# Token sums of the output projection: eight router products and four sums of squares per group of four blocks instead of three products per block

## The chip, the cores and the metric

The kernel runs on one NeuronCore of one Trainium2 chip. The metric is the device time of one execution in microseconds; the median of three runs of the kernel before is 2050.81 us (2050.77, 2050.81 and 2059.14).

## The reference, cut to what matters

Two layers (`DEPTH = 2`) work on 256 context tokens and 256 latent tokens of width 1024. Each layer has a token mixer, which ends in an output projection, and an expert-choice mixture of 16 experts. What the experts need of a token is its root mean square and its router affinity, both sums over all 1024 channels of the stream that leaves the mixer:

```python
def rms_norm(x, g):
    xf = x.astype(jnp.float32)
    y = xf * lax.rsqrt(jnp.mean(xf * xf, axis=-1, keepdims=True) + EPS)
    return (y * g.astype(jnp.float32)).astype(x.dtype)

def modulate(x, g, shift, scale):
    return rms_norm(x, g) * (1 + scale) + shift

def expert_choice_moe(h, router, w1, w3, w2):
    cap = CAPACITY_FACTOR * L // N_EXPERTS
    aff = jax.nn.softmax((h @ router).astype(jnp.float32), axis=-1)
    g, idx = lax.top_k(aff.transpose(0, 2, 1), cap)
    ...
```

The second layer drops the context, so its mixer and its experts end in 256 tokens where the first has 512.

## The kernel before, in words

The stream x is held transposed: a block is 128 channels on the partitions, with 512 tokens (context and latents) in the free dimension, or 256 in the second layer. There are KB = 8 such blocks.

**Output projection** (lines 1356 to 1376). For each block d, `load` (line 791) brings the 128 columns `wo{d}` of the output matrix, 512 KB, into one of three raw buffers, ScalarE copies its high part (L798) and VectorE subtracts to get the low part (L799), into one of two pairs of buffers. TensorE then runs 24 products, three for each of eight k, into a PSUM tile of tag "d" (`pd` in the rows): 128x512 in the first layer, 128x256 in the second. VectorE adds the result, times the modulation, to x (L1372), once for each stream. Then `pre.step(d)` takes what the experts need of this block.

**Token sums** (`TokenSums`, line 534, used by `MoePre`, line 587). For block k, `step` issues one router product for each stream, [128 channels, 32] against x, 256 tokens, into 32 partitions of PSUM tile `pr` (`pm` in the rows); a square of x on ScalarE (L550); and one product of a matrix of ones with the square, 512 or 256 tokens, into 32 partitions of PSUM tile `p2` (`pa` in the rows). Which 32 partitions, and with it which column group of the array, depends on the block:

```python
q, r = (k % 4, 4) if ns == 1 else (2 * s + k % 2, 2)
j = 32 * (k % 4)
```

These products are plain float32, which the trace shows as two rows each. `tokens` (line 553) copies both tiles out (L558, L560) and adds the four groups up in small products. From there VectorE makes 1/rms, softmax and top-k (L576, L500 to L504, L1399 to L1424), and the gather of the experts' tokens starts. The same class runs once more, without a router, at the end of the first layer's experts (L1657 and L1659), for the norm of the second mixer; its `p2` has tag "s" there (`ps` in the rows).

**Experts** (`moe`, line 1386). Their weights come as 384 tiles of 1 MB (two of the last matrix by columns), issued by SyncE in one queue (L1565), first come first served, into whatever buffers are free; a tile is issued when the products that read the buffer before are done. Some buffers are free during the output projection, six in a region that was just given back, others when the projection's own operands and x's helpers are released. The DMAs of `wo{d}` (L797) are in the same queue.

Matmuls of all helpers are recorded at L428, transposes at L425. The order of each engine's instructions is set by a scheduler from the program and its own estimate of times, not by hand.

Of the kernel before, what the change touches and what calls it, by code (L numbers as in the profile page):

```python
# [19 lines left out]
KB = 8  # L20
NE = 16
CAP = 32
EPS = 1e-6
RA, RB = 12288, 12288                            # columns of the two regions that change type with the phase
BASE = 52736 - RA - RB
ENGS = ('AV', 'AVG')                             # engines of the copies of q and k, by layer
# steps of the modulation (by layer, of which parts may be left over) among the other work
TR = (0, 2, 0.5)                                 # at the end of the experts, before and among the second mixer's h
SCN = (0.5, 0.5)                                 # per level of a scan
FL = (1, 1)                                      # the rest before the merge  # L30
DAS = (0.5, 1)                                   # per head and query block
ADA = (2, 2)                                     # per block of w_in
FIRST = ("gk", "gq")                             # blocks of the second mixer loaded during the experts
AHEAD = ((0, 0), (0, 5))                         # tiles of experts loaded during the mixers


# ---------------------------------------------------------------- layouts
# [21 lines left out]
LATE = CN.at["adab"][0]                          # those from here on give way to weights of the experts  # L59
C0 = Pack()                                      # needed at the start only  # L60
# [104 lines left out]
def dft():  # L165
    """Transforms at the odd frequencies 2 pi (k + 1/2) / 512, k < 256, where no wrapped term meets the 511 of the
    convolution. Phases are counted from the middles of the signal, 127.5, of the filter's tap 128, and of the
    outputs 128..383; cosines are then even and sines odd in t <-> 255 - t, and half of the t will do."""
    th = 2 * np.pi * (np.arange(256) + 0.5) / 512
    a = np.outer(np.arange(256) - 128, th)  # L170
    filt = np.concatenate([np.cos(a), -np.sin(a)], 1)
    a = np.outer(np.arange(128) - 127.5, th)
    fwd = np.concatenate([np.cos(a), -np.sin(a)], 1)
    inv = np.concatenate([np.cos(a.T), np.sin(a.T)], 1) / 256
    two = lambda m: m.reshape(2, 128, -1).transpose(1, 0, 2).reshape(128, -1)
    return np.concatenate([two(filt), fwd, two(inv)], 1).astype(np.float32)


def pack_inputs(a):
    """Layout of the inputs; every element is a copy of an input's element or a constant of the shapes."""  # L180
# [50 lines left out]
    for l in range(2):  # L231
# [5 lines left out]
        wb = a["w_branch"][l].reshape(4, 2, 128, 2, 4, 128)          # i, k, p, half, d, n  # L237
        for i in range(4):
            for h in range(2):
                wg[l, BIDX[f"wb{i}{h}"]] = wb[i, :, :, h].transpose(1, 2, 0, 3).reshape(128, 8, 128)   # p, (d, k), n  # L240
# [10 lines left out]
# ---------------------------------------------------------------- device  # L251
class Mem:
    """Columns of one SBUF tile, those longest free first; Tile sees which bytes each instruction touches."""
# [7 lines left out]
    def take(self, n, avoid=None):  # L261
        """avoid: first and last + 1 of columns not to be touched."""
# [39 lines left out]
    def merge(self):  # L302
        """Joins neighbouring free runs (their stamps become the latest)."""
# [8 lines left out]
    def cut(self, b, n):  # L312
        """Gives the first n columns of b back; the rest stays."""
# [12 lines left out]
class Buf:  # L326
# [3 lines left out]
    def __call__(self, off=0, dims=None, p0=0, np_=128, n=None):  # L330
        """AP of rows p0..p0+np_, from column off, free dims [[stride, count], ...]."""
# [19 lines left out]
def build(tc, ins, outT, dbg=None, stop=None):  # L351
# [30 lines left out]
    # ---------------- persistent  # L382
    cn = mem.take(CN.n)
    sm = mem.take(SM.n)                              # of the layer
    cs_b = mem.take(256)
    mod = [mem.take(96) for _ in range(2)]          # [6 chunk, 8 k, 2 stream]
    xb = [mem.take(4096), 0]                         # [stream, k, 256]; columns cut off in front
    x_at = xb[0].at
    NR = 3
    raws = [mem.take(1024) for _ in range(NR)]       # blocks of the mixers' weights as they come  # L390
# [45 lines left out]
    # ---------------- adaLN  # L436
    def load_c(c):
        """silu(c) of both streams, 32 columns for each block of 128."""
# [17 lines left out]
    class Ada:  # L456
        """Streams ada_w[l] in tiles of one k-block of a 1024-column chunk."""
# [17 lines left out]
    class AdaBack:  # L475
        """The same in the background, in two buffers of its own."""
# [6 lines left out]
        def run(self, n=None):  # L483
            """n: steps, or parts of one."""
# [12 lines left out]
    # ---------------- little helpers  # L497
    def rsqrt_small(x, n, y, t):
        """y = x ** -0.5 on n columns (x, y, t: functions of nothing giving APs)."""
# [6 lines left out]
    def rms_rows(l, t0, mem=mem, nsq=3):  # L506
        """1/rms over d of x, on every partition: PSUM [128, 512 - t0]."""
# [26 lines left out]
    class TokenSums:  # L534
        """Sums over d while x comes block by block: x^2, and x against a [d, 16] matrix per stream."""
# [6 lines left out]
        def step(self, k):  # L542
            W, b, ns = 512 - self.t0, self.sq[k % len(self.sq)], self.ns
            j = 32 * (k % 4)
            if self.AR:
                for s in range(ns):
                    ss = s + 2 - ns
                    q, r = (k % 4, 4) if ns == 1 else (2 * s + k % 2, 2)
# [1217 lines left out]
```

## Time and profile before

| | |
|---|---|
| median of three runs | 2050.81 us |
| span of the profiled execution, first to last instruction | 2046.6 us |
| the median less that span | 4.2 us |
| TensorE matmul busy | 1883.5 us (92%) |
| VectorE busy | 801.6 us (39%) |
| ScalarE busy | 525.8 us (26%) |
| bytes moved by DMA | 549.03 MB, mean 268 GB/s |

The profile comes from one execution; beside its span no further time of that execution is recorded, so the 4.2 us around it are the difference to the median run. A busy TensorE means that a matmul is in the pipeline, not that it is used to the full. Rows of the trace give the start in microseconds from the first instruction, the length, engine, source line, operation, out<-in by the program's names, the shape (rows*columns of the array, then the operand that streams through), and how many instructions the row merges. A float32 product is two such instructions, a product of the projection's split parts one.

### The profile page before, as it was taken

To read this page: it belongs to the slowest core of one execution; us is meant where nothing else is said; L and a number is where in the kernel's file an instruction comes from. 1 tells how busy PE (TensorE), PEld (TensorE's weight loads), DVE (VectorE), ACT (ScalarE), POOL (GpSimd) and SP (SyncE) were. 2 spreads that over 40 slices of the span, in tenths; PEclk is the share of its full clock that TensorE was granted. 3 is DMA by queue.
4 is the path that set the end of the run, shared out by engine and by line. 5 is a ranking of instruction groups with operands and counts; after the bars stand their busy time and mean duration, and the time that the engine had idled before them with its cause. 6 is when DMAs were issued, how large, how long until landed. Compare 5 with 4: busy or idle time off the path is not lost.

```text
span 2046.6 us, 28476 instructions
## 1 busy us (share of the span) xinstructions
PE 1883.5 (92%) x11722; PEld 1091.5 (53%) x11722; DVE 801.6 (39%) x1768; ACT 525.8 (26%) x929; POOL 27.4 (1%) x52
## 2 busy tenths in 40 slices
PE   7999999999999799999887899999998999997877
PEld 3666677887886434434232356888996433231213
DVE  5455648747442323212120245769864111010101
ACT  4433336622231211101000243447442100000000
POOL 0000000000000000000000010001000000000000
PEclk9989999999999899999999999999999999999999
DMA  7734521222335799999999855324577999999999
GB/s 306 231 128 145 185 95 63 93 92 74 134 121 219 293 388 386 351 409 409 409 409 409 320 201 194 106 95 143 196 257 287 388 409 409 409 409 409 409 409 331
DMA packets 154005, 549.03 MB, mean 268 GB/s; under 512 B 11026, under 2 KB 22674, under 8 KB 153108
## 3 DMA queue, kind: packets, MB, share of 16 engines
q1 hardware_dynamic: 153300, 544.08, 70.3%
q0 software_dynamic: 576, 3.15, 0.4%
q8 instruction: 92, 1.51, 0.3%
q14 instruction: 37, 0.30, 0.0%
HBM read 544.03 MB, written 3.15 MB: 267 GB/s over the span
## 4 chain that ended last, share of the span: by engine, by line
PE 72%; DMA 18%; DVE 5%; issue 3%; ACT 2%; SPq 0%; DVEq 0%; ACTq 0%
PE pd L428 42%; PE ps L428 15%; DMA r<-moe_w 8%; PE pm L428 7%; DMA base<-moe_w 6%; PE pa L428 6%; DMA base<-ada_w 2%; PE pm L425 2%; DMA base<-wg 1%; PE ps L1591 1%; ACT r L798 1%; DVE r L799 1%; DMA base<-xT 0%; PE ps L425 0%; DVE r L1189 0%
## 5 line engine op out<-in xcount | busy, mean ns | idle before, releaser
L428 PE MATMUL pd<-r 128*128 128x256 f32 (+3 forms) x2976 | 582.8, 365 | 11.2 <-DMA r<-moe_w 6.7
L428 PEld LDWEIGHTS pd<-r 128*128 128x128 f32 (+2 forms) x2976 | 424.9, 184 | 146.1 <-issue 73.1
L428 PE MATMUL pd<-r,r 128*128 128x512 f32 (+3 forms) x1304 | 282.5, 433 | 12.1 <-DMA r<-moe_w 9.4
L799 DVE TENSOR_TENSOR r<-base,r 128x1024 fp32r<-128x1024 f32 x136 | 165.8, 1221 | 159.7 <-ACT r L798 156.5
L428 PEld LDWEIGHTS pd<-r,r 128*128 128x128 f32 (+2 forms) x1304 | 161.8, 166 | 107.0 <-issue 58.3
L798 ACT ACTIVATE r<-base 128x1024 fp32r<-128x1024 f32 x136 | 143.3, 1058 | 283.1 <-PE pd L428 224.2
L428 PE MATMUL ps<-base 32*64 32x64 f32 (+12 forms) x2372 | 176.7, 278 | 13.2 <-DMA base<-hy 4.8
L428 PE MATMUL pd<-r,base 128*32 128x512 f32 (+1 forms) x680 | 167.8, 599 | 13.5 <-DMA r<-moe_w 11.5
L428 PEld LDWEIGHTS ps<-base 32*64 32x64 f32 (+7 forms) x2372 | 112.4, 142 | 74.2 <-issue 42.2
L428 PE MATMUL pm<-base 128*128 128x128 f32 (+12 forms) x660 | 112.8, 327 | 18.9 <-issue 11.6
L428 PE MATMUL ps<-r,base 128*64 128x512 f32 (+4 forms) x468 | 98.6, 525 | 13.5 <-DVE base L1592 6.3
L428 PEld LDWEIGHTS pm<-base 128*128 128x128 f32 (+5 forms) x660 | 73.8, 180 | 66.1 <-issue 38.6
L428 PE MATMUL pd<-base 128*32 128x512 f32 (+1 forms) x408 | 101.4, 596 | 6.4 <-DMA base<-moe_w 5.6
L428 PEld LDWEIGHTS pd<-r,base 128*32 128x32 f32 (+1 forms) x680 | 42.0, 122 | 113.7 <-issue 74.4
L1588 DVE TENSOR_TENSOR r<-base,pd 64x512 f32<-64x512 f32 x16 | 10.9, 680 | 212.6 <-PE pd L428 212.6
L1587 ACT ACTIVATE base<-pd 128x512 f32<-128x512 f32 (+1 forms) x32 | 19.0, 594 | 253.9 <-PE pd L428 253.9
L1588 DVE TENSOR_TENSOR base<-base,pd 128x512 f32<-128x512 f32 x16 | 11.0, 687 | 185.7 <-PE pd L428 151.5
L428 PE MATMUL pa<-r,r 128*128 128x512 f32 (+1 forms) x384 | 82.6, 342 | 1.1 <-DVE base L860 1.1
L428 PE MATMUL pa<-base 128*32 128x256 f32 (+1 forms) x704 | 74.6, 399 | 7.7 <-DMA base<-ada_w 7.5
L428 PE MATMUL pd<-base,r 128*32 128x512 f32 (+1 forms) x296 | 71.3, 597 | 9.4 <-DMA base<-moe_w 9.4
L1638 ACT ACTIVATE base<-ps 32x512 f32<-32x512 f32 (+2 forms) x28 | 14.7, 525 | 253.8 <-PE ps L428 249.4
L1638 ACT ACTIVATE r<-ps 32x512 f32<-32x512 f32 (+2 forms) x32 | 15.3, 479 | 247.6 <-PE ps L428 242.1
(241 smaller groups left out, 1636.2 us busy)
## 6 DMA issues: line engine op xcount, KB each, us to landing
r<-moe_w SPq DMA_DIRECT2D x251, 1024.0 KB, 18.1
base<-moe_w SPq DMA_DIRECT2D x131, 1024.0 KB, 17.7
base<-wg SPq DMA_DIRECT2D x152, 512.0 KB, 3.3
base<-ada_w SPq DMA_DIRECT2D x84, 512.0 KB, 4.6
r<-ada_w SPq DMA_DIRECT2D x12, 512.0 KB, 10.7
base<-xT SPq DMA_DIRECT2D x4, 1024.0 KB, 6.5
filters<-r SPq DMA_DIRECT2D x8, 256.0 KB, 4.0
base<-filters POOLq DMA_DIRECT2D x2, 1024.0 KB, 6.6
```

What stands on the lines that cost most here:

```text
L425: T.transpose(out, in_, ident)
L428: return T.matmul(out, lhsT, rhs, start=start, stop=stop, **kw)
L798: A.activation(w[0](), raw(), AF.Copy)
L799: V.tensor_tensor(w[1](), raw(), F(w[0]()), op=OP.subtract)
L1587: A.activation(s_(np_=rows), pa[0:rows, :], AF.Silu)
L1588: V.tensor_tensor(h_(np_=rows), s_(np_=rows), pb[0:rows, :], op=OP.mult)
L1591: T.transpose(p[:, q * rows:q * rows + rows], h_(q * 128, n=128, np_=rows), cs("ident", n=rows, np_=rows))
L1638: A.activation(dst, src, AF.Copy)
```

## The change

`TokenSums.step` no longer issues products for every block. It squares the block, and at every fourth block issues the router products of four blocks in a row and then the four sums of squares in a row. `MoePre` holds four buffers of squares instead of two. Results and the number of products are the same. (Comments and docstrings also go, and lines behind 541 move by six.)

```diff
         def step(self, k):
-            W, b, ns = 512 - self.t0, self.sq[k % len(self.sq)], self.ns
-            j = 32 * (k % 4)
-            if self.AR:
-                for s in range(ns):
-                    ss = s + 2 - ns
-                    q, r = (k % 4, 4) if ns == 1 else (2 * s + k % 2, 2)
-                    mm(self.pr[32 * q:32 * q + 32, 0:256], self.AR(k * 64 + ss * 32, n=32), xk(k, ss), k < r, k >= KB - r)
+            W, b, ns = 512 - self.t0, self.sq[k % 4], self.ns
             A.activation(b(0, n=W) if self.t0 else b(0, [[256, 2], [1, 256]]), xks(k, self.t0), AF.Square)
-            mm(self.p2[j:j + 32, 0:W], cs("ones", n=32), b(0, n=W), k < 4, k >= 4)
+            if k % 4 < 3:
+                return
+            four = range(k - 3, k + 1)
+            if self.AR:
+                for i in four:
+                    for s in range(ns):
+                        ss = s + 2 - ns
+                        q, r = (i % 4, 4) if ns == 1 else (2 * s + i % 2, 2)
+                        mm(self.pr[32 * q:32 * q + 32, 0:256], self.AR(i * 64 + ss * 32, n=32), xk(i, ss), i < r, i >= KB - r)
+            for i in four:
+                j = 32 * (i % 4)
+                mm(self.p2[j:j + 32, 0:W], cs("ones", n=32), self.sq[i % 4](0, n=W), i < 4, i >= 4)
...
-            self.sq = [mem.take(512 - t0) for _ in range(2)]
+            self.sq = [mem.take(512 - t0) for _ in range(4)]
```

What the scheduler makes of it, at three places. First TensorE in the first layer's output projection, blocks 0 to 2, before (`pd` are the projection's products, `pm` router products, `pa` sums of squares):

```order
L428 MATMUL pd_4695<-r_227 128x512 x3
L428 MATMUL pm_4657<-base 32x256 x2
L428 MATMUL pd_4695<-r_227 128x512 x3
L428 MATMUL pa_4656<-base 32x512
L428 MATMUL pd_4695<-r_227 128x512 x18
L428 MATMUL pd_4729<-r_227 128x512 x3
L428 MATMUL pm_4657<-base 32x256
L428 MATMUL pd_4729<-r_227 128x512 x2
```

and now, from block 3's products on:

```order
L428 MATMUL pd_4754<-r_227 128x512 x24
L428 MATMUL pm_4657<-base 32x256 x7
L428 MATMUL pa_4656<-base 32x512
L428 MATMUL pm_4657<-base 32x256
L428 MATMUL pa_4656<-base 32x512 x3
L428 MATMUL pd_4797<-r_227 128x512 x24
```

The three products of a block stood some products deep in the next block's; now all twelve of four blocks stand right behind block 3's last product, and the same twelve again behind block 7's, ahead of the transposes.

Second TensorE at the end of the first layer's experts, where `ps_6689` is the tile of the sums (the other `ps` are the last expert's products, `pm` the scatter, `pa` the modulation). Before:

```order
L428 MATMUL ps_6689<-base 32x512 x2
L428 MATMUL ps_6699<-r_4938,base 64x128 x16
L428 MATMUL ps_6689<-base 32x512
L428 MATMUL pm_6727<-r_4934 128x256 x2
L428 MATMUL ps_6734<-r_4938,base 64x64 x16
L428 MATMUL pm_6755<-r_4934 128x256 x2
```

and now:

```order
L428 MATMUL ps_6689<-base 32x512 x2
L428 MATMUL ps_6734<-r_4938,base 64x64 x3
L428 MATMUL ps_6689<-base 32x512
L428 MATMUL ps_6734<-r_4938,base 64x64 x13
L428 MATMUL ps_6689<-base 32x512
L428 MATMUL pm_6755<-r_4934 128x256 x2
```

Here the scheduler pulls the sums apart again: two in a row, one, one, and further down (not shown) two, one, one; before it was two, one, one, one, one and two.

Third SyncE's queue in the first layer's output projection (`wg` is a block of the projection's matrix, `r_4934` the region that is free by then, `r_4938` and the later `base` are buffers that the projection itself gives back). Before:

```order
L1565 DMA r_4934<-moe_w 128x2x1024 x2
L797 DMA base<-wg 128x1024
L1565 DMA base<-moe_w 128x2x1024 x4
L1565 DMA r_4938<-moe_w 128x2x1024 x2
L1565 DMA base<-moe_w 128x2x1024 x2
L1565 DMA r_4938<-moe_w 128x2x1024 x4
```

and now:

```order
L803 DMA base<-wg 128x1024
L1571 DMA r_4934<-moe_w 128x2x1024
L1571 DMA base<-moe_w 128x2x1024 x4
L1571 DMA r_4938<-moe_w 128x2x1024
L1571 DMA base<-moe_w 128x2x1024 x2
L1571 DMA r_4938<-moe_w 128x2x1024 x5
```

One tile for `r_4938` has moved behind the two tiles for `base`. In the second layer it is the same: one tile for the region, one for `base` and five for the region before, two for `base` and six for the region now.

## Rows read from the trace of the kernel before

**Rows 1.** The page: the chain that ended last, by engine (q: its sequencer).

```profile
PE 72%; DMA 18%; DVE 5%; issue 3%; ACT 2%; SPq 0%; DVEq 0%; ACTq 0%
```

**Rows 2.** Busy time by stretch: PE, PEld, DVE, ACT, POOL, granted clock, DMA share, GB/s.

```profile
38.00:42.00 4.00, 3.45 (x66) 1.86 (x54) 3.60 (x10) 0.00 (x0) 0.00 (x0) 1.00 1.02 410
...
640.00:672.00 32.00, 32.00 (x123) 19.02 (x122) 7.18 (x11) 5.71 (x7) 0.00 (x0) 1.00 0.26 106
...
684.00:694.00 10.00, 3.61 (x13) 2.73 (x13) 7.19 (x26) 0.00 (x0) 0.00 (x0) 0.50 1.02 412
```

**Rows 3.** Busy time by stretch of the projection's products (tile pd) alone, layer by layer.

```profile
612.18:672.42 60.24, 47.64 (x188) 33.90 (x188) 6.13 (x14) 0.00 (x0) 1.00 0.50 198
1537.82:1571.14 33.32, 26.60 (x192) 23.71 (x192) 3.38 (x7) 0.37 (x1) 1.00 0.75 285
```

**Rows 4.** Chain of waits: undisturbed 24 products, first and second layer.

```profile
596.13 5.50 PE pd L428 x24
...
1527.23 2.87 PE pd L428 x24
```

**Rows 5.** TensorE in time, first layer's output projection: sum of squares, router product.

```profile
619.49 1.04 PE L428 MATMUL pa<-base 128*32 128x512 f32 x2
620.46 5.06 PE L428 MATMUL pd<-r 128*128 128x512 f32 x21
625.45 0.62 PE L428 MATMUL pm<-base 128*32 128x256 f32 x2
626.00 0.73 PE L428 MATMUL pd<-r 128*128 128x512 f32 x2
```

**Rows 6.** Chain of waits: 32 modulation products, 32 columns each, four column groups in turn.

```profile
37.70 3.63 PE pa L428 x64
```

**Rows 7.** VectorE in time: residuals, low part, copy of the sums, first step behind them.

```profile
656.71 0.88 DVE L1372 SCALAR_TENSOR_TENSOR base<-pd,base 128x256 f32<-128x256 f32 x2 [5.63 <-PE pd L428]
...
672.63 0.88 DVE L1372 SCALAR_TENSOR_TENSOR base<-pd,base 128x256 f32<-128x256 f32 x2 [6.91 <-PE pd L428]
676.97 0.69 DVE L558 COPY base<-pa 128x512 f32<-128x512 f32 x1 [3.46 <-PE pa L428]
...
1541.93 1.22 DVE L799 TENSOR_TENSOR r<-base,r 128x1024 fp32r<-128x1024 f32 x1 [0.53 <-ACT r L798]
...
1571.35 0.48 DVE L1372 SCALAR_TENSOR_TENSOR base<-pd,base 128x256 f32<-128x256 f32 x1 [3.87 <-PE pd L428]
1574.02 0.42 DVE L558 COPY base<-pa 128x256 f32<-128x256 f32 x1 [2.18 <-PE pa L428]
```

**Rows 8.** ScalarE in time: square in the first layer, high part and square in the second.

```profile
657.67 0.63 ACT L550 ACTIVATE base<-base 128x512 f32<-128x512 f32 x1
...
1540.84 1.06 ACT L798 ACTIVATE r<-base 128x1024 fp32r<-128x1024 f32 x1 [1.11 <-PE pd L428]
1541.80 0.40 ACT L550 ACTIVATE base<-base 128x256 f32<-128x256 f32 x1
```

**Rows 9.** SyncE's queue in time: weight tiles of the experts.

```profile
672.63 0.88 SPq L1565 DMA_DIRECT2D r<-moe_w  x2
678.85 0.88 SPq L1565 DMA_DIRECT2D base<-moe_w  x2
...
703.78 8.95 SPq L1565 DMA_DIRECT2D r<-moe_w  x6
...
1571.34 0.37 SPq L1565 DMA_DIRECT2D r<-moe_w  x1
1575.64 0.37 SPq L1565 DMA_DIRECT2D base<-moe_w  x1
```

**Rows 10.** The page: DMA issues, KB each, median us from issue to landing.

```profile
base<-wg SPq DMA_DIRECT2D x152, 512.0 KB, 3.3
```

**Rows 11.** TensorE in time, end of the first layer's experts: two sums in a row.

```profile
1161.62 1.37 PE L428 MATMUL ps<-base 128*32 128x512 f32 x4
1162.92 1.97 PE L428 MATMUL ps<-r,base 128*64 128x128 f32 x32
```

More of the change, by code (lines that the diff above doesn't have):

```diff
@@ L542, in step @@
         def step(self, k):
-            W, b, ns = 512 - self.t0, self.sq[k % len(self.sq)], self.ns
-            j = 32 * (k % 4)
-            if self.AR:
-                for s in range(ns):
-                    ss = s + 2 - ns
-                    q, r = (k % 4, 4) if ns == 1 else (2 * s + k % 2, 2)
-                    mm(self.pr[32 * q:32 * q + 32, 0:256], self.AR(k * 64 + ss * 32, n=32), xk(k, ss), k < r, k >= KB - r)
-            A.activation(b(0, n=W) if self.t0 else b(0, [[256, 2], [1, 256]]), xks(k, self.t0), AF.Square)
-            mm(self.p2[j:j + 32, 0:W], cs("ones", n=32), b(0, n=W), k < 4, k >= 4)
+            W, b, ns = 512 - self.t0, self.sq[k % 4], self.ns
+            A.activation(b(0, n=W) if self.t0 else b(0, [[256, 2], [1, 256]]), xks(k, self.t0), AF.Square)
+            if k % 4 < 3:
+                return
+            four = range(k - 3, k + 1)
+            if self.AR:
+                for i in four:
[6 more added lines that the diff above has]
+                mm(self.p2[j:j + 32, 0:W], cs("ones", n=32), self.sq[i % 4](0, n=W), i < 4, i >= 4)
         def tokens(self, mem):
```

## The prediction
> **What bounds the kernel now.** I read the chain of waits first: TensorE holds 72% of it, DMA 18% [rows 1]. So the question for each place that the change touches is whether TensorE or the stream of experts' weights sets its end. Then I read the output projection of either layer in order of time. TensorE is the bound there: in the first layer 188 of its 192 products lie between 612.18 and 672.42, with no idle time on TensorE [rows 2, 3]. Undisturbed, 24 such products take 5.50 us, 0.229 each [rows 4]; 188 take 43.1 us, and the stretch is 60.24 us. The other 17.1 us are the token sums of seven blocks (14 router products, 7 sums of squares; block 8's lie behind the stretch). In the second layer 192 products at 2.87/24 = 0.1196 us make 23.0 of 33.32 us [rows 3, 4], and 10.4 us go to 14 products (one router product and one sum per block), 0.74 each. Last I read SyncE's queue, since a stage that ends earlier helps only if the weights come earlier too. From 640 to 672 the DMAs are busy for 0.26 of the time, and the next tiles are issued at 672.63, when the projection's buffers come free [rows 2, 9]. In 684 to 694 they are at 1.02 [rows 2]. So the stream stands still until the projection ends and then runs full: it moves with that end.
>
> **What a product costs alone and in a group.** A router product standing alone takes 0.55 us from its start to that of the next projection product (625.45 to 626.00), a sum of squares 0.97 (619.49 to 620.46) [rows 5]. The modulation's 32-column products, whose four column groups follow each other, run 32 in 3.63 us: 0.113 each, four in 0.45 [rows 6]. They are float32 with 256 columns like the router products, and all their moving operands differ. I read this as four products running side by side, each holding its own group for 0.45 us; a first-layer sum, with 512 columns, holds it for 0.91. Of the 17.1 us, 14 x 0.45 + 7 x 0.91 = 12.7 is that work done one after the other; 4.4 is going in and out of 21 interruptions, 0.2 each.
>
> **First layer, first group of twelve.** It stands right behind block 3's products. Per column group it has two router products and one sum: 2 x 0.45 + 0.91 + 0.2 = 2.0 us if nothing waits. One after the other it would be 8 x 0.45 + 4 x 0.91 + 0.2 = 7.4. I take a value near the lower end, as rows 6 have the same shape, but the last sum needs block 3's square, and no other products stand ready behind it: residuals from 656.71, square from 657.67, over at 658.30 [rows 7, 8], so 1.6 us after the block's end, then 0.91 and 0.2, and 0.1 for the handover, as between the residual's end at 657.59 and the square: 2.8 us. Gain 17.1 - 2.8 = 14.3, between 9.7 and 15.1.
>
> **First layer, second group.** Before, 4.34 us passed from block 7's residual (672.63) to the copy of the sums (676.97), with transposes ahead of sums on TensorE and their copies ahead of the square on ScalarE [rows 7]. Now residuals 0.88, square 0.63, sum 0.91 and three handovers of 0.1 make 2.7; gain 1.6. The transposes come later; they are hidden by top-k, during which TensorE is busy for 3.6 of 10 us [rows 2], but the exponential of the softmax now has most of their copies ahead of it on ScalarE. I take 1.4, between 0 and 1.6. The tile that moved behind `base`: before, `base` was issued 6.2 us after the residual's start; 1.4 less is 4.8. Nine tiles follow, 1.05 MB at 412 GB/s or 2.55 us each, and 2.0 us for the first to get going (512 KB land 3.3 us after their issue, of which 1.3 is the transfer at that rate) [rows 10]: done at 29.8. The queue then waits for the first expert's buffers, at 31.2 before (703.78) [rows 9], 29.8 now. It fits exactly, so I cost it at nothing; if it is late, it costs up to 2.55.
>
> **Second layer.** The first group is three router products and one sum, then the last router product with two sums, then, four projection products later, the last sum alone. With the residual (0.48) in between, the first part is 1.6 us past what the projection would take; the lone sum is 0.74 as before: 2.4 (all side by side 2 x 0.45 + 0.2 = 1.1, one after the other 8 x 0.45 + 0.2 = 3.8). Gain 10.4 - 2.4 = 8.0, between 6.6 and 9.3. This needs weights at a faster pace: high and low part are ready 2.3 us after a block's end (1540.84 to 1541.93 + 1.22) [rows 7, 8], a block now takes 2.87; 0.5 us of cover. At the end, 2.67 us (1571.35 to 1574.02) become 0.48 + 0.40 + 0.45 + 0.3 = 1.6: gain 1.0. But here the tile issued at 1571.34 goes behind the one at 1575.64 [rows 9], and the stream starts later against the projection's end: I take 0.9 back, between 0 and 2.55.
>
> The Trainium skill, page "TensorE: Matmul & The Clock Gate", section "Part 3: Packing small matmuls — row/col tiling", gives 2.38 times for three column tiles, so 79% of full overlap. An estimate from that figure: the side-by-side parts (1.8 us in the first layer, 0.9 in the second) would be 0.5 and 0.2 longer in each of two groups, the gain 1.4 smaller and the time 2027.8. Rows 6 show no such loss, four in 0.45 against one in 0.55, so the sum goes by them.
>
> **End of the first layer's experts.** Eight sums stand among scatter products. Two in a row take 1.30 us (1161.62 to 1162.92) [rows 11], one alone 0.97. The order now has one pair more and two single ones less: 2 x 0.97 - 1.30 = 0.6 gained. A sum that waits for its square would cost about one single sum: between -1.0 and 1.9. The doubled square buffers cost nothing by themselves: the squares are the same instructions.
>
> **Sum.** 14.3 + 1.4 + 8.0 + 1.0 - 0.9 + 0.6 = 24.4 us. Against the profiled span, 2046.6 becomes 2022.2; with the 4.2 us around it, that is the median of 2050.8 becoming **2026.4**.
>
> **Rivals.**
> - *The products do not overlap* (the change does not do what it says). For: in these stages no row shows more than two such products side by side. Against: rows 6. Then the groups cost 7.4 and 3.8. The gain is 9.7 + 6.6 in the projections; the ends lose 3.1 (7.4 against 4.3) and 1.2 (3.9 against 2.7); 0.9 is taken back: 11.1 left, 2039.7. Chance 0.06.
> - *The weight stream gives a tile back*: the moved tile is late in both layers, 2.55 instead of 0 and of 0.9. For: full DMAs once they start, and my sum fits without slack. Against: the queue still waits for buffers afterwards. Gain 20.2, 2030.6. Chance 0.10.
> - *The second projection waits for its weights*: its blocks cannot come faster than loads that share the queue with 1 MB tiles. The 8.0 us go, 2034.4. For: only 0.5 us of cover. Against: loads are issued several blocks ahead. Chance 0.05.
> - *The clock falls, and it is slower than before*: TensorE stands still while the first group waits, and full groups of narrow products come without projection products between; if the granted clock went to 1.2 GHz for blocks 4 to 7, 96 products at 0.229 more and 96 at 0.12 more cost 33.5 us: 9.1 slower, 2059.9. It decides once it holds for 73% (24.4/33.5) of those blocks. For: 0.50 in 684 to 694, with little work. Against: 1.00 through 640 to 672, and through 38 to 42, where such narrow products are most of the work [rows 2]. Chance 0.03.
>
> **How the numbers follow.** The forecast has 0.76. About 0.5%, 10.3 us, is what a measurement of this kernel can tell from no change. Faster by more: 0.76 + 0.10 + 0.05 and half of the first rival, which lies at that bound, 0.94; within it 0.03; slower 0.03. The best ends of all terms (15.1, 1.6, 9.3, 1.0, 1.9) make 28.9 us, 2021.9; the range begins at 2021.5. Upwards it takes in the second rival and part of the way to the third, 2033.0; left out are the first, third and fourth, 0.14.
>
> **What would show it.** In the first layer blocks 1 to 3 and 5 to 7 run 5.5 us each without a gap; behind block 3 twelve products take about 2.8 us with the last waiting for the square; the copy of the sums begins about 2.7 us after block 7's residual; SyncE issues the first tile at about 658. In the second layer the stretch of 33.3 us is about 25. The granted clock stays at 1.00 through both. Wrong would be: twelve products that take near 7 us; gaps between projection products that wait for high or low parts; a first expert that starts early but waits for a tile; a gain that is seen at 690 and gone at 1150, where the weights of the first layer end.

## The result, and the profile after

Five executions of the changed kernel have a median of **2031.1 us** (2021.9 to 2033.1), beside 2050.8 of the kernel before: ratio 0.990, 95% interval 0.9871 to 0.9928, so 19.7 us by the medians. A second set of five, run later beside eleven of the kernel before, has 2020.5 beside 2053.3: ratio 0.9843, interval 0.9818 to 0.9868, 32.8 us. The forecast was 24.4 us, 2026.4. The first set's 2031.1 lies in the range that was given, 2021.5 to 2033.0; the second set's 2020.5 lies 1.0 us below it. The two sets differ by more than their intervals, though the kernel is the same. The first experiment shows what differs, and reads the change in two ways that depend on it less: 27.0 us by the pieces of the program that it touches, 25.3 us by the whole span at an equal granted clock.

The profiled execution of the changed kernel (own time 2021.9) is the fastest of its set. The page, with its span, the granted clock in 40 slices, and the chain by engine:

```profile
span 2020.1 us, 28474 instructions
...
PEclk9998999999999899999999999999998999999999
...
PE 71%; DMA 20%; DVE 5%; issue 2%; ACT 2%; SPq 0%; DVEq 0%; ACTq 0%
```

TensorE still holds the chain; its share fell by a point and that of the DMAs rose by two [rows 1], since the stages that shrank are TensorE's. Busy time by stretch of the projection's products (tile pd), both layers, columns as in [rows 3]:

```profile
610.28:656.08 45.80, 43.16 (x188) 35.13 (x188) 6.13 (x14) 0.00 (x0) 1.00 0.68 261
1520.43:1545.70 25.27, 23.63 (x192) 23.12 (x192) 3.39 (x7) 0.00 (x0) 1.00 0.94 364
```

60.24 became 45.80 us and 33.32 became 25.27, for the same 188 and 192 products, at a granted clock of 1.00 in both. The DMA share rose from 0.50 to 0.68 and from 0.75 to 0.94: the projection's weights now come in less time. TensorE in time in the first layer (the start of a row, its length; each float32 product has two records, so x16 in all are eight router products and x8 four sums):

```profile
610.30 21.19 PE L428 MATMUL pd<-r 128*128 128x512 f32 x92
631.42 1.27 PE L428 MATMUL pm<-base 128*32 128x256 f32 x14
632.31 0.59 PE L428 MATMUL pa<-base 128*32 128x512 f32 x1
...
632.74 1.44 PE L428 MATMUL pa<-base 128*32 128x512 f32 x5
634.11 22.05 PE L428 MATMUL pd<-r 128*128 128x512 f32 x96
```

92 products without a gap, the group of twelve from 631.42 to 634.11, 2.69 us, then 96 without a gap. The second layer has its group in two parts, with four projection products and a lone sum behind it:

```profile
1532.06 0.63 PE L428 MATMUL pm<-base 128*32 128x256 f32 x6
...
1533.27 0.74 PE L428 MATMUL pd<-r 128*128 128x256 f32 x4
1533.94 0.62 PE L428 MATMUL pa<-base 128*32 128x256 f32 x2
1534.49 11.29 PE L428 MATMUL pd<-r 128*128 128x256 f32 x92
```

VectorE in time: two residuals in the middle of the first layer, then the last residual and the copy of the sums in either layer (compare [rows 7]):

```profile
639.88 0.88 DVE L1378 SCALAR_TENSOR_TENSOR base<-pd,base 128x256 f32<-128x256 f32 x2 [6.21 <-PE pd L428]
645.32 0.88 DVE L1378 SCALAR_TENSOR_TENSOR base<-pd,base 128x256 f32<-128x256 f32 x2 [3.30 <-PE pd L428]
...
656.20 0.88 DVE L1378 SCALAR_TENSOR_TENSOR base<-pd,base 128x256 f32<-128x256 f32 x2 [4.56 <-PE pd L428]
658.93 0.69 DVE L564 COPY base<-pa 128x512 f32<-128x512 f32 x1 [1.86 <-PE pa L428]
...
1545.82 0.48 DVE L1378 SCALAR_TENSOR_TENSOR base<-pd,base 128x256 f32<-128x256 f32 x1 [2.39 <-PE pd L428]
1547.84 0.42 DVE L564 COPY base<-pa 128x256 f32<-128x256 f32 x1 [1.53 <-PE pa L428]
```

Blocks that run on without sums between them follow each other by 5.44 us (639.88 to 645.32). From the last residual to the copy it takes 2.73 us in place of 4.34, and 2.02 in place of 2.67. SyncE's queue in time, the experts' weights:

```profile
656.19 0.37 SPq L1571 DMA_DIRECT2D r<-moe_w  x1
658.29 3.37 SPq L1571 DMA_DIRECT2D base<-moe_w  x2
...
685.86 8.95 SPq L1571 DMA_DIRECT2D r<-moe_w  x6
```

The first tile is issued when the projection ends; the queue waits for the first expert's buffers until 685.86, 29.7 us after the residual, where it was 31.2 before [rows 7, 9].

### The profile page after: what moved, and what is told of

Read it like the earlier page. It is cut to its first block, busy times and chain, and to the rows that moved or that the text cites. A ratio compares the mean times of both kernels' runs of the same rounds, so it can differ in the third digit from the quotient of the medians.

```text
span 2020.1 us, 28474 instructions
## 1 busy us (share of the span) xinstructions
PE 1859.6 (92%) x11722; PEld 1089.5 (54%) x11722; DVE 801.5 (40%) x1768; ACT 526.1 (26%) x929; POOL 28.7 (1%) x52
## 4 chain that ended last, share of the span: by engine, by line
PE 71%; DMA 20%; DVE 5%; issue 2%; ACT 2%; SPq 0%; DVEq 0%; ACTq 0%
PE pd L428 41%; PE ps L428 15%; DMA r<-moe_w 9%; DMA base<-moe_w 7%; PE pm L428 6%; PE pa L428 6%; DMA base<-ada_w 2%; PE pm L425 2%; DMA base<-wg 1%; ACT r L804 1%; PE ps L1597 1%; DVE r L805 1%; DMA base<-xT 0%; DVE r L1195 0%; DVE base L1594 0%
## 5 line engine op out<-in xcount | busy, mean ns | idle before, releaser
L428 PE MATMUL pd<-r 128*128 128x256 f32 (+3 forms) x2976 | 572.3, 363 | 12.0 <-DMA r<-moe_w 7.6
L428 PE MATMUL pd<-r,base 128*32 128x512 f32 (+1 forms) x680 | 166.7, 598 | 12.0 <-DMA r<-moe_w 10.4
L428 PE MATMUL pm<-base 128*128 128x128 f32 (+12 forms) x660 | 104.7, 326 | 18.3 <-DVE base L1528 5.8
L428 PE MATMUL pa<-base 128*32 128x256 f32 (+1 forms) x704 | 70.1, 407 | 9.4 <-DMA base<-ada_w 9.2
## 6 DMA issues: line engine op xcount, KB each, us to landing
r<-ada_w SPq DMA_DIRECT2D x12, 512.0 KB, 10.3
```

What stands on the lines that cost most here:

```text
L428: return T.matmul(out, lhsT, rhs, start=start, stop=stop, **kw)
```

## The experiments

Five pieces of the program hold the stages that the change touches, and every run below is read by them: in either layer from block 0's first residual to block 7's (VectorE, starts), from there to the copy of the sums, and from the last expert's second products in the first layer (TensorE) to the copy of the sums behind them (VectorE). In us:

| kernel | layer 1, residuals | to the copy | experts' end | layer 2, residuals | to the copy | sum |
|---|---|---|---|---|---|---|
| before | 55.52 | 4.34 | 26.41 | 30.44 | 2.67 | 119.4 |
| before, again | 55.54 | 4.34 | 26.42 | 30.44 | 2.67 | 119.4 |
| changed | 40.99 | 2.73 | 24.32 | 22.29 | 2.02 | 92.4 |
| changed, again | 40.99 | 2.73 | 24.32 | 22.27 | 2.02 | 92.3 |
| one column group | 44.06 | 5.74 | 25.45 | 23.92 | 3.57 | 102.7 |
| late group | 40.18 | 2.68 | (28.44) | 21.34 | 2.02 | |
| projections only | 41.00 | 2.73 | 26.43 | 22.29 | 2.02 | 94.5 |
| router products only | 48.68 | 3.79 | 26.43 | 26.86 | 2.51 | 108.3 |
| sums only | 49.91 | 4.64 | 24.32 | 26.77 | 2.50 | 108.1 |
| late group, halves | 40.18 | 2.45 | 24.32 | 21.34 | 2.02 | 90.3 |

The piece in brackets fell into a stretch of lower granted clock (last section). Blocks are counted from 0 as in the code; an expectation that speaks of block 8, or of block 1's first residual, counts from 1. Diffs are against the changed kernel where nothing else is said.

### The same two kernels again

No edit. Of the changed kernel this was put down:

> The changed kernel once more, unaltered, to tell the change from the scatter of single executions. If the gain is local to the two projections and their ends, the stretch of the first projection is 45.8 us again (within 0.2), that of the second 25.3, the group of twelve 2.7. The parts that the change does not touch tell the scatter: if the 1.9 us before the first projection (612.2 to 610.3) and the 2.5 us given back in the second mixer (352.7 to 355.2 from its first instruction to its projection) come from the change, they stand here again; if they are scatter, they come out otherwise by 1 us or more. The median stays within 5 us of 2031.1.

and of the kernel before:

> The kernel before once more. The pieces that the change touches come out as in its first profile within 0.1 us: 55.5 us from first to last residual in the first layer, 4.3 to the copy of the sums, 26.4 from the last expert's second products to the copy of the sums, 30.4 and 2.7 in the second layer. The start of the first projection and the length of the second mixer differ from the first profile by some us and follow the granted clock of their stretches. If the second mixer is 361 us again with the same dips of the clock as in the changed kernel's profiles (361.7 to 364.4), the change costs something there that it does not explain.

Measured: every piece repeats within 0.03 us, for either kernel. What lies between does not: block 0's first residual in the first layer begins at 615.21 in the changed kernel's first profile and at 609.64 in its second; at 617.11 and 612.87 in those of the kernel before. Busy time by stretch, with the granted clock third from the right; first the changed kernel:

```profile
120.00:140.00 20.00, 20.00 (x362) 14.24 (x358) 16.65 (x35) 5.39 (x9) 0.00 (x0) 0.91 0.27 85
140.00:160.00 20.00, 19.33 (x244) 14.11 (x242) 13.33 (x27) 9.45 (x22) 2.17 (x4) 0.91 0.40 133
180.00:200.00 20.00, 17.91 (x203) 10.56 (x203) 11.31 (x24) 4.20 (x8) 1.92 (x2) 0.83 0.61 196
```

then the same kernel's second profile:

```profile
120.00:140.00 20.00, 19.27 (x370) 13.86 (x368) 17.45 (x37) 5.76 (x9) 0.00 (x0) 1.00 0.29 85
140.00:160.00 20.00, 19.65 (x247) 14.50 (x246) 12.25 (x25) 9.91 (x23) 2.48 (x5) 1.00 0.41 133
180.00:200.00 20.00, 19.06 (x246) 12.67 (x248) 10.63 (x22) 5.31 (x11) 1.92 (x2) 1.00 0.58 187
```

The work is the same and the clock is not. At the granted share, TensorE loses at most 20 x (0.09 + 0.09 + 0.17) = 7.0 us in these three stretches; the second profile starts its first projection 5.6 us earlier, and from 40 us up to there its clock is 1.00 throughout. So the 1.9 us by which the first projection of the changed kernel began earlier than before are no part of the change, nor are the 2.5 us by which its second mixer took longer: from the experts' end to the second layer's first residual it takes 360.9 and 363.8 us in the two profiles of the kernel before, 363.5 and 364.4 in those of the changed one. What of the first set's 19.7 and the second's 32.8 us is the change's can't be read from medians of five. The pieces give 27.0 us.

The executions as a whole can be read too, once their clock is allowed for. For 88 executions, those of the changed kernel, of the kernel before beside the experiments, and of the kernels below, both the span and the mean granted clock are on record. A straight line through them, with a level of its own for each kernel in each set, falls by 2.0 us for each 0.001 of mean clock, and the spans scatter around it by 2.1 us (an estimate from these numbers). At a mean clock of 0.986 the changed kernel spans 2022.3 us in its first set and 2022.6 in its second, the kernel before 2047.4 and 2048.0 in two sets: the difference is 25.3 us, give or take 1.5. So the two sets of the changed kernel agree once their clock (median 0.983 and 0.989) is allowed for. Below, "at an equal clock" means this reading. It does not match the pieces for every kernel, and differences of 1 to 4 us between the two stay unexplained.

### One column group for all

```diff
-                for i in four:
-                    for s in range(ns):
+                for s in reversed(range(ns)):
+                    for i in four:
...
-                        mm(self.pr[32 * q:32 * q + 32, 0:256], self.AR(i * 64 + ss * 32, n=32), xk(i, ss), i < r, i >= KB - r)
+                        mm(self.pr[64 * s:64 * s + 32, 0:256], self.AR(i * 64 + ss * 32, n=32), xk(i, ss), i == 0, i == KB - 1)
...
-                mm(self.p2[j:j + 32, 0:W], cs("ones", n=32), self.sq[i % 4](0, n=W), i < 4, i >= 4)
+                mm(self.p2[0:32, 0:W], cs("ones", n=32), self.sq[i % 4](0, n=W), i == 0, i == KB - 1)
```

`tokens` then reads those rows of 32 alone.

> Groups of four blocks as in the changed kernel, but the products of a group stand in one column group (the router products of the two streams of the first layer in one each, one stream after the other). Theory A, the products of a group run side by side because each has its own column group: then here they go one after the other, the first layer's group takes 8 x 0.45 + 4 x 0.91 + 0.2 = 7.4 us in place of 2.7 and its projection 50.5 in place of 45.8; in the second layer 8 x 0.45 + 0.2 = 3.8 in place of 2.3, the stretch 26.8 in place of 25.3; the ends lose 4.5 and 1.9, the end of the first layer's experts some 2: about 14 us over the changed kernel, 2045. Theory B, what counts is only how often the projection is interrupted: the groups cost 2.7 and 2.3 as in the changed kernel, the time is 2031.

Measured: median 2033.1 of six, 12.6 us over the changed kernel's 2020.5 in the same set where some 14 were expected (ratio to before 0.9908, interval 0.9887 to 0.9929). The second layer is the clean case, since every product of its group is in one column group. TensorE in time there:

```profile
1531.96 1.91 PE L428 MATMUL pm<-base 128*32 128x256 f32 x8
1533.71 1.89 PE L428 MATMUL pa<-base 128*32 128x256 f32 x8
1535.53 11.78 PE L428 MATMUL pd<-r 128*128 128x256 f32 x96
```

Four router products take 1.75 us, four sums 1.82: 0.44 and 0.45 each, one after the other, 3.57 for the group. In the first layer the two streams' router products and the sums still had two column groups between them, and the built order put two sums among the first four router products, which are of the other group, so that part of it ran side by side; what stands alone at the end of the group shows the single prices:

```profile
628.24 1.89 PE L428 MATMUL pm<-base 128*32 128x256 f32 x8
629.97 1.88 PE L428 MATMUL pa<-base 128*32 128x512 f32 x4
631.77 22.07 PE L428 MATMUL pd<-r 128*128 128x512 f32 x96
```

Four router products in 1.73, two sums in 1.80. The group from 626.04 to 631.77 is 5.73 us in place of 2.69; with 7.4 I had counted no overlap at all. The first column group alone has four router products and four sums, 4 x 0.43 + 4 x 0.90 = 5.3 us, and that is most of it. Theory B asked for 2.7 and falls; theory A stands for the groups, while the ends lost less than it asked for (3.0 and 1.6 us in place of 4.5 and 1.9). By the pieces 10.4 us of the 27.0 are lost with the column groups, at an equal clock only 6.8 (give or take 2). The rest stays; it can come from going in and out less often, from waits that fall away, and from the overlap that was left here, which this run does not separate.

### The first group one block later

```diff
-            if k % 4 < 3:
+            if k not in (3 + self.late, KB - 1):
                 return
-            four = range(k - 3, k + 1)
+            four = range(4) if k < KB - 1 else range(4, KB)
...
-            self.sq = [mem.take(512 - t0) for _ in range(4)]
+            self.sq = [mem.take(512 - t0) for _ in range(5)]
```

> The group of blocks 0 to 3 is issued behind block 4's products in place of block 3's (with a fifth square buffer), so that no product of it waits for a residual or a square; the group at the end and the sums among the experts stay. Theory A1, the group of twelve takes 2.7 us because its last sum waits for block 3's square: here it takes 2 x 0.45 + 0.91 + 0.2 = 2.0 and the first projection 45.1; in the second layer 2 x 0.45 + 0.2 = 1.1 in place of 2.3, the projection 24.1: 1.9 us less in all, 2029, to be seen in the trace and not in the median. Theory A2, the work of the group itself fills the time (the side by side running loses a part): the stretches stay at 45.8 and 25.3.

`late` is 1 in the two projections and 0 in the sums among the experts, which stay as they were; the squares go through the buffers in turn.

Measured: TensorE in time, the group of the first layer and that of the second:

```profile
637.21 1.07 PE L428 MATMUL pm<-base 128*32 128x256 f32 x16
638.10 1.04 PE L428 MATMUL pa<-base 128*32 128x512 f32 x8
639.07 16.63 PE L428 MATMUL pd<-r 128*128 128x512 f32 x72
...
1545.38 0.64 PE L428 MATMUL pm<-base 128*32 128x256 f32 x8
1545.84 0.61 PE L428 MATMUL pa<-base 128*32 128x256 f32 x8
1546.38 8.89 PE L428 MATMUL pd<-r 128*128 128x256 f32 x72
```

Twelve products in 1.86 us (2.0 expected), eight in 1.00 (1.1 expected), and the layers' pieces are 0.81 and 0.95 shorter. Eight router products take 0.89, about as long as two in one column group (2 x 0.43), and four sums 0.97, as long as one alone [rows 5]. So A1 holds: what the changed kernel's group has beyond that is the wait for block 3's square. The median is 2025.4 of six (ratio 0.9876, interval 0.9853 to 0.9899), which does not tell it from the changed kernel, as expected. At an equal clock it spans 2024.0 us, no less than the changed kernel's 2022.5: the 1.8 us are seen in the pieces and not in the whole.

### The experts' end as it was

```diff
+            self.g = 4 if AR else 1
...
-            if k % 4 < 3:
+            if k % self.g < self.g - 1:
                 return
-            four = range(k - 3, k + 1)
+            four = range(k - self.g + 1, k + 1)
```

> The groups of four only in the two projections; the eight sums among the scatter products at the end of the first layer's experts stand singly, each behind its square, as in the kernel before. If the 2.1 us gained there (17.8 us early at the last expert's second products, 19.9 at the copy of the sums) come from the grouped sums, that piece is 2.1 us longer here than in the changed kernel; if they are scatter or come from the earlier arrival, it stays. If the 2.5 us given back in the second mixer come from the new order of the sums among the modulation's steps, the second mixer up to its projection takes 352.7 here in place of 355.2; else it does not care. The time is that of the changed kernel within 3 us.

Measured: that piece is 26.43 us, as in both profiles of the kernel before, and 24.32 wherever the sums are grouped with a column group for each, save in the one execution whose clock fell there: the 2.1 us are the change's. TensorE in time, first with the sums single (this run), then grouped (the changed kernel):

```profile
1144.08 1.10 PE L428 MATMUL pm<-r 128*128 128x256 f32 x4 [0.62 <-DVE base L1656]
1145.11 1.37 PE L428 MATMUL ps<-base 128*32 128x512 f32 x4
```

```profile
1145.93 1.05 PE L428 MATMUL ps<-base 128*32 128x512 f32 x4
1146.91 0.45 PE L428 MATMUL ps<-r,base 128*64 128x64 f32 x6
...
1154.34 1.89 PE L428 MATMUL ps<-base 128*32 128x512 f32 x4
1156.16 1.13 PE L428 MATMUL pm<-r 128*128 128x256 f32 x4
```

Singly, TensorE stands still for 0.62 us before a row of scatter products, until a residual on VectorE (L1656) is done; in the changed order that wait is gone. Two sums in a row take 0.98 in place of 1.30, fully side by side, but the next pair takes 1.82: its second sum waits for its square (ScalarE makes it from 1154.52 to 1155.13, behind a high part of the next mixer's weights, and the sum starts at 1155.19). The second mixer up to its first residual takes 362.6 us here. Over all profiles it is 360.9 to 363.8 us in four with the sums single and 361.7 to 367.5 in six with the sums grouped. The dips of the clock differ from one to the next; taking off the share that the grant withheld, by 20 us stretches, leaves 356.7 to 359.2 and 356.7 to 360.6 (an estimate). So no sign is left that the order of the sums matters there.

The time at an equal clock, 2022.7 us, is that of the changed kernel; the 2.1 us of this piece are not seen in it.

### Each half of the change alone

Router products only, and sums only:

```diff
-            if k % 4 < 3:
-                return
-            four = range(k - 3, k + 1)
-            if self.AR:
+            four = range(k - k % 4, k + 1)
+            if self.AR and k % 4 == 3:
...
-            for i in four:
+            for i in [k]:
```

```diff
-            if k % 4 < 3:
-                return
-            four = range(k - 3, k + 1)
+            four = range(k - k % 4, k + 1)
             if self.AR:
-                for i in four:
+                for i in [k]:
...
-            for i in four:
+            for i in four if k % 4 == 3 else []:
```

> Only the router products wait for their group of four blocks; each sum of squares stands singly behind its own square as in the kernel before. From block 1's first residual to block 8's the first layer took 55.5 us before and 41.0 in the changed kernel, the second 30.4 and 22.3. Theory A (a product holds its column group for its own time, whoever holds the others, plus 0.2 for each interruption): the sums keep 7 x 0.97 = 6.8 of the 17.1 us, the routers' 10.3 become 2 x 0.45 + 0.2 = 1.1: 46.3; second layer 30.4 less 7 x 0.74 = 5.2, plus 0.45 + 0.2: 25.9. Rival R (the many short router products are the whole loss, since each one interrupts): nearly all of the gain comes, 42 and 23.

> Only the sums of squares wait for their group of four; the router products of each block stand singly as in the kernel before. Theory A: the routers keep 10.3 of 17.1 us, the sums' 6.8 become one group whose last waits for block 4's square, 2.7: 55.5 - 4.1 = 51.4 in the first layer; second layer 30.4 - 5.2 + 1.6 = 26.8. The two halves of the change then add up: 9.2 + 4.1 = 13.3 beside 14.5 measured for both, 4.5 + 3.6 = 8.1 beside 8.1. Rival R: next to nothing is gained here in either layer, 55 and 30.

Measured: 2041.3 and 2040.8 (ratios 0.9947 and 0.9951, intervals 0.9923 to 0.9972 and 0.9925 to 0.9977): each half gives about half, and rival R falls. In the second layer 3.58 and 3.67 us were gained (4.5 and 3.6 expected), in the first 6.8 and 5.6 (9.2 and 4.1 expected). The first layer's split was off, for a reason in each half. TensorE in time with the sums single:

```profile
615.83 1.05 PE L428 MATMUL pa<-base 128*32 128x512 f32 x2
616.81 5.74 PE L428 MATMUL pd<-r 128*128 128x512 f32 x24
622.48 1.04 PE L428 MATMUL pa<-base 128*32 128x512 f32 x2
```

A block with a sum takes 6.65 us (615.83 to 622.48), where a block that runs on takes 5.44: the sum costs 1.21, since the 24 products behind an interruption take 5.67, 0.23 more. I had put 0.97 for the sum, without that restart: 7 x 0.24 = 1.7 us of the 2.4 by which this half fell short. The rest lies at block 3, where the built order puts the last router product behind a projection product by itself. With the router products single:

```profile
614.30 0.98 PE L428 MATMUL pm<-base 128*32 128x256 f32 x4
615.21 5.73 PE L428 MATMUL pd<-r 128*128 128x512 f32 x24
```

Two router products of one block, one for each stream, have column groups of their own and yet take 0.91 together. The second starts some 0.36 late: its stream's residual ends at 614.61 (two in 0.88 us from 613.73 on VectorE). Even so the pair, with the restart, costs less than the 10.3/7 = 1.47 us that I had put: in four of the six intervals between residuals without a group it comes to 6.57 or 6.58 - 5.44 = 1.1, and to 1.5 in the two where the built order separates the pair. Both halves together give 14.53 in the first layer, 2.1 more than the two gains added. That would fit what the halves share: when one kind of product goes, the other still interrupts at every block.

### Block 7's square and sum in halves

Against the late group:

```diff
+            halves = self.AR and ns == 2 and k == KB - 1
+            if halves:
+                for s in range(2):
+                    A.activation(b(s * 256, n=256), xk(k, s), AF.Square)
...
+                n = 256 if halves and i == k else W
+                for c in range(0, W, n):
+                    mm(self.p2[j:j + 32, c:c + n], cs("ones", n=32), self.sq[i % len(self.sq)](c, n=n), i < 4, i >= 4 and c + n == W)
```

> The late first group, and in the first layer block 8's square and sum in two halves of 256 columns, one for each stream, so that the first half runs while the second stream's residual and square are made. If the tail is the chain residual, square, sum: from block 8's residual to the copy of the sums 0.88 + 0.1 + 0.35 + 0.1 + 0.45 + 0.2 = 2.1 in place of 2.7. Rival: a half square costs nearly what a whole one does and stands behind the other on ScalarE, the tail stays at 2.6. The projections are those of the late group, 40.2 and 21.3 us from first residual to last.

Measured: the tail is 2.45 us, between the two. ScalarE in time, the two squares; VectorE, residual and copy; TensorE, the last router product (two records) and the last sums:

```profile
654.95 0.81 ACT L549 ACTIVATE base<-base 128x256 f32<-128x256 f32 x2 [4.42 <-DVE base L1386]
```

```profile
654.43 0.88 DVE L1386 SCALAR_TENSOR_TENSOR base<-pd,base 128x256 f32<-128x256 f32 x2 [4.56 <-PE pd L428]
656.88 0.69 DVE L572 COPY base<-pa 128x512 f32<-128x512 f32 x1 [1.58 <-PE pa L428]
```

```profile
655.36 0.40 PE L428 MATMUL pm<-base 128*32 128x256 f32 x1
...
655.60 0.38 PE L428 MATMUL pm<-base 128*32 128x256 f32 x1
655.64 1.21 PE L428 MATMUL pa<-base 128*32 128x512 f32 x7
```

Two half squares take 0.81 us where a whole one takes 0.63, so the second is done at 655.76. The first half's sum could start at some 655.4, but its column group, the fourth, is held by block 7's last router product, which waited for the second residual and runs from 655.36 to 655.82. So both half sums run behind it, four records some 0.216 apart from 655.82 on, by the end of their row, and only the squares' 0.2 us come off the chain. The median is 2023.5 of six, ratio 0.9853 (0.9817 to 0.9888). By the pieces this version has 2.1 us less than the changed kernel and is the shortest of all; the medians, 7.6 us apart from one set of the changed kernel and 3.0 the other way from the other, can't show it, and at an equal clock it spans 2023.0 us beside 2022.5.

## Why the prediction was right, step by step

- **Products side by side.** Right, and the single prices with it: 0.45 for a router product and 0.91 for a sum were read from modulation products [rows 6]; one behind the other in one column group they take 0.43 and 0.90, and twelve that wait for nothing 1.86, or 2.10 with the restart behind them, where I had 2.0 in all. The Trainium skill, page "TensorE: Matmul & The Clock Gate", section "Part 3: Packing small matmuls — row/col tiling", gives 2.38 times for three column tiles, from which the estimate was 0.5 us more in each first-layer group. The trace does not agree: 2 x 0.43 + 0.90 = 1.76 us would be full overlap and some 2.2 that share of it (an estimate), and 1.86 were measured in the late group.
- **First layer's projection.** 14.3 forecast, 14.4 by the stretches (60.24 to 45.80). The group of twelve took 2.69 us up to the next product and 2.9 with the restart, where I had 2.8, and it waits for the square, as the later group shows. One term was read too high: the 5.50 us of [rows 4] for 24 products is a row's length, while blocks that run on follow each other by 5.44. That puts the token sums at 17.6 us before, not 17.1, and what is left of them at 3.2 now; the difference hardly moves.
- **First layer's end.** 4.34 became 2.73, 1.6 of gain; 1.4 was put down because transposes move behind the sums. Of the 1.6, 1.5 are left at the end of the queue's wait for the first expert's buffers. The tile that moved in SyncE's queue cost nothing: the queue's wait for the first expert's buffers ends 29.7 us after the residual where 29.8 was forecast.
- **Second layer's projection.** 8.0 forecast, 8.05 by the stretches. No row there waits for weights, though the DMA share is 0.94: the 0.5 us of cover was enough.
- **Second layer's end.** Mis-sized twice, in opposite ways. The gain to the copy is 0.65 in place of 1.0: the square ends at 1546.82 and the lone last sum, which stands behind a transpose, starts at 1547.18, 0.36 us later where I had put 0.1 for a handover. The 0.9 taken back for the late tile did not come: from the copy of the sums to the end of the program it takes 472.6 and 474.2 us in the two profiles of the kernel before, 472.3 and 472.6 in those of the changed one.
- **Experts' end.** 2.1 us in place of 0.6, and beyond the bound of 1.9. My step priced the sums alone (one pair more, two single ones less). It left out the 0.62 us of TensorE's wait in front of a scatter product, which lies on that path and which the new order removes, and scatter products that now run in longer rows: from start to start of TensorE's rows the 32 of them take 8.1 us in place of 8.9. The sums, with the modulation products among them, gave 1.0, and the last expert's products, now cut apart, took 0.3 back.
- **The sum.** 24.4 forecast; by the pieces 119.4 - 92.4 = 27.0, of which 2.1 - 0.6 = 1.5 and the 0.9 are the two terms above. The first set's medians show 19.7, the second's 32.8, the spans at an equal clock 25.3. My range was made of the ends of the terms alone and had nothing for the scatter of executions, which moved the median of one kernel by 10.6 us between two sets. That the first median fell into it is in part luck: the second, of the same kernel, is outside.
- **The rivals.** No overlap: the kernel that takes the column groups away shows what it would have been like, and the change is not that. A tile given back, or weights that hold the second projection up: no row of TensorE in the projections or at the first expert's start waits for a DMA. A fall of the clock in the first projection: it is 1.00 from 610 to 656.

## What to carry to other kernels

Narrow products among the products of a stage that TensorE bounds cost three times: their own time, here 0.2 to 0.3 us of going in and out, and whatever the last of them waits for. Gather as many as there are column groups, give each its own, and issue them where their operands have long been ready: then eight cost what two do (0.89 us beside 0.86). Issuing the first group one block late gained 1.8 us in the pieces here, but no gain of the whole was shown for it. Read such a change by the pieces that it touches, since these repeat within 0.03 us where medians of the whole moved by ten, and check their sum against spans at an equal granted clock.

## What the runs showed that was not expected

Most of the scatter between executions of one kernel goes with the granted clock, which falls in places that no edit touches. Of the first set's five executions of the changed kernel the one with a mean clock of 0.985 spans 2020.1 us, that with 0.984 2028.2, the three with 0.983 2026.3 to 2030.7. The late group's profiled execution shows one such place in a row. TensorE in time, the last expert's second products, late group:

```profile
1139.52 3.68 PE L428 MATMUL ps<-base 128*64 128x128 f32 x32 [0.78 <-DVE base L1599]
```

and the same products with the change in the projections only:

```profile
1137.04 1.97 PE L428 MATMUL ps<-base 128*64 128x128 f32 x32 [0.78 <-DVE base L1599]
```

1.87 times as long, in a stretch of 20 us with a mean grant of 0.66, between the two levels of 1.2 and 2.4 GHz; a last tile of weights that came late (2.16 us of waiting) stands ahead of it, but so it does in the changed kernel's second profile (2.18 us), where the clock stays at 1.00. In that execution the experts' end took 28.4 us in place of 24.3, and the execution 2034.7 where four of its six took 2023.5 to 2025.4. What makes the clock fall in one execution and not in the next stays open: no run was made for it.

The second thing is small. A column group that is held counts as a wait like any other: of two products that are ready, the one whose group is busy stands back, and since the order on TensorE is fixed, a router product that waits for its residual can hold up a sum that is ready. The last experiment shows it once: the half sum that could start at some 655.4 ran from 655.82.
